# Rotary attention scores on one core: loads that wait for the transposes, a rotation ahead of a copy, an earlier GpSimd drain and fewer semaphores

## The chip, the cores and the metric

One core of one Trainium2 chip runs the kernel. The metric is the device time of one execution in microseconds. Three timed runs of the kernel before gave 801.99, 803.25 and 803.15 us; the median is 803.15.

## The reference

q and k are [16 batches, 512 positions, 16 heads, 64] in float32. Both are rotated by position (rotary embedding), and then the scores of each batch and head are formed between all pairs of positions. The output is [16, 512, 16, 512] float32, which is 268 MB; q and k together are 67 MB.

```python
q_rot = np.concatenate([q1 * cos - q2 * sin, q1 * sin + q2 * cos], axis=-1)   # q1, q2: halves of the last axis
k_rot = np.concatenate([k1 * cos - k2 * sin, k1 * sin + k2 * cos], axis=-1)
scores = np.einsum('bshd,bthd->bsht', q_rot, k_rot)
```

## The kernel before

**Tiles.** A batch of q or of k is one tile of 128 partitions x 4 slots x 1024 numbers (2048 KB); partition p holds positions 4p to 4p+3, and slot c is position 4p+c of all partitions. Two buffers for q and two for k stand in SBUF (`in_t`, L134). The unit of the main loop is one slot of q, numbered i = 4 x batch + slot, 64 in all. For each i the kernel forms all 16 heads' scores in eight head pairs p = 0 to 7 and writes 4096 KB to the output.

**One pass of the main loop (L461 to L485).** TensorE (PE) multiplies a pair's transposed q by the batch's transposed k (`scores`, L343, matmuls on L358). ScalarE (ACT) copies the result out of PSUM into one of three staging buffers (L370), and after the eighth pair SyncE (SP) issues the store of the staging buffer (L382). Between the pairs PE transposes later slots: q's slot i+1 after pairs 1 and 3, k's slot i+4 after pairs 5 and 6 (`transposed`, L287, on L299). VectorE (DVE) copies q's transposes out of PSUM and ACT those of k (L317). DVE rotates q's slot i+2 after pair 3 and k's slot i+5 at the end of the pass (`rope`, L237: three instructions, a product with cos on L275, one with sin in place on L276, their sum on L277). Once a batch DVE copies three of four transposed slots of the next k (kN) into the working k (kT) in two halves: `renew(0)` after pair 3 and `renew(1)` at the end (L325 to L336).

**The first batch (L423 to L458)** is done in another order: its inputs come early in small pieces, its stores are 16 of 1024 KB, and at the end of its last pass (i = 3, L452 to L457) DVE has three things in a row: `renew(1)`, which must wait until PE has made the last pairs of batch 0 since it overwrites their k; the rotation of q's slot 5; and the rotation of k's slot 8.

**Loads.** After pass i with i % 4 = 2 the load of q's batch i/4 + 2 is issued, after i % 4 = 3 that of k's batch i/4 + 3 (L482 to L485). Most go to SP's queue, right behind the store of the same pass, and SP is the only engine that issues stores. Five loads are RELIEVED (L188): q's batches 6, 11 and 15 and k's batches 7 and 12. These are issued by GpSimd (POOL), 120 partitions in 8 KB pieces, with tiny transfers (`move_cursor`) in front that shift which DMA engine takes what; the other 8 partitions go in 2 KB pieces through ACT's queue (q) or POOL's (k) (`load_around`, L199). In the profile SP's queue is q1, POOL's q0, ACT's q10.

**Waits.** `Plan.add` (L30) records which operation reads and writes which key and gives each operation the waits that are not implied by earlier ones; an engine's operations stay in the order in which they are added. A load writes the keys of its tile, so it waits for the tile's readers. The readers on record are the DVE rotations alone: the last is the sum (L277) of the tile's slot 3. Loads on SP's queue stand behind a store which waits for ACT, which is later than all of that; for the five loads on POOL this wait is the one that counts. `place` (L153) gives each operation's semaphore site, one for each engine, parity of i, kind and pair; the PE loop of the main passes counts them up by one a turn.

**The end (L507 to L509).** SP waits for the last stores; POOL waits for the tiny transfers. Then the frame of the program makes each engine drain and meet the others twice, with a clearing of the semaphores by POOL in between (shown at L550).

Of the kernel before, what the change touches and what calls it, by code (L numbers as in the profile page):

```python
# [94 lines left out]
def kernel(  # L95
# [57 lines left out]
    def place(engine, *where):  # L153

        i = now[0]
        return (engine,) + ((i % 2,) + where if i >= C else ("first",))

    def turn():
        i = now[0]
        return (i - FIRST) // 2 if FIRST <= i < FIRST + 2 * TURNS else None  # L160

    def work(engine, fns, reads, writes, *where, aside=False):
        t = turn() if engine == "PE" else None
        plan.add(engine, fns, reads, writes, site=place(engine, *where), turn=t, aside=aside)

# [33 lines left out]
    def load_around(which, b, t, keys, site):  # L199
        n, SMALL = 120, E // 8  # L200
        x = RELIEVED[which, b]
        d = dram[which][b]

        def pieces(queue, lo, hi, F, key, sem):
            m = E // F
            src = bass.AP(d.tensor, d.offset + lo * E + E - F, [(E, hi - lo), (-F, m), (1, F)])
            v = t[lo:hi].rearrange("p c e -> p (c e)")
            dst = bass.AP(v.tensor, v.offset + E - F, [v.ap[0], (-F, m), (1, F)])
            transfer(queue, dst, src, [], [key], sem)

        if x == 0:
            plan.add("POOL", [lambda: nc.gpsimd.inc_swdge_sem([], [], mode="reset_dge_cursor")])
        else:
            move_cursor(16 - SLOW)
        if x % 2:
            move_cursor(8)
            pieces("POOL", n, P, SMALL, keys[1], site + ("rest",))
        move_cursor(SLOW + 1)
        pieces("POOL", 0, n, E // 2, keys[0], site)
        if not x % 2:  # L220
            pieces("ACT", n, P, SMALL, keys[1], site + ("rest",))
# [4 lines left out]
    def load(which, b):  # L226
        if b >= B:
            return
        t, keys = in_t[which, b % 2], in_keys(which, b)
        site = ("in", which, b % 2)  # L230
        if (which, b) in RELIEVED:
            load_around(which, b, t, keys, ("around", which, b))
        else:
            transfer("SP", t.rearrange("p c (h d) -> p c h d", h=H), dram[which][b], [], keys, site)

# [51 lines left out]
    def transposed(which, n, g, engine):  # L287
        j = banks[0] % 2
        banks[0] += 1
        bank = ps_t[j]  # L290
        fns = []
        for x in range(4):
            if n < C:
                src = units[which, n][0][:, x, P * g : P * (g + 1)]
                key = ("unit", which, n)
            else:
                src = rot[which][:, P * (4 * g + x) : P * (4 * g + x + 1)]
                key = ("rot", which)
            fns.append(lambda x=x, src=src: nc.tensor.transpose(bank[:, x, :], src, ident))  # L299
        work("PE", fns, [key, "ident"], [("bank", j)], which, g)  # L300
        src = bank
        if which == "q":
            dst, keys = qT[n % 2][:, 4 * g : 4 * g + 4, :], [("qT", n % 2, g)]
        elif n < C:
            dst = kT[:, 2 * n + g].rearrange("p (t c) -> p t c", c=C)
            src = bank.rearrange("p c t -> p t c")
            keys = [("kT", 2 * n + g, x) for x in range(2)]
        elif n % C < C - 1:
            dst = kN[:, 4 * g : 4 * g + 4, P * (n % C) : P * (n % C + 1)]
            keys = [("kN", n % C, g)]  # L310
        else:
            dst = kT[:, 4 * g : 4 * g + 4, S - P : S]
            keys = [("kT", 4 * g + x, 1) for x in range(4)]

        def copy():
            f = nc.scalar.copy if engine == "ACT" else nc.vector.tensor_copy
            work(engine, [lambda: f(out=dst, in_=src)], [("bank", j)], keys, "out", which, g)  # L317

        return copy
# [23 lines left out]
    def scores(i, p):  # L343
        j = RING[HP * (i % 2) + p]
        s = stage_of(i)
        ps, st = ps_s[j], stage[s]
        b = i // C
        if b == 0:
            c, hp = divmod(p, 2)
            lhs, chunk, g = qT[i % 2][:, C * hp + c], 2 * i + hp, hp  # L350
        else:
            lhs, chunk, g = qT[i % 2][:, p], p, p // 4
        rhs = kT[:, chunk]
        fns = []
        for r in range(2):
            a = slice(64 * r, 64 * r + 64)
            fns.append(
                lambda r=r, a=a: nc.tensor.matmul(  # L358
                    out=ps[:, r, :], lhsT=lhs[a, :], rhs=rhs[a, :], start=True, stop=True
                )  # L360
            )
        work("PE", fns, [("qT", i % 2, g), ("kT", chunk, 0), ("kT", chunk, 1)], [("ps", j)], "pair", p)
        so, si = st[:, 2 * p : 2 * p + 2, :], ps
        if b > 0:
            so = so.rearrange("s r (t c) -> s r t c", c=C)
            si = si.rearrange("s r (c t) -> s r t c", c=C)
        writes = [("st", s, p)]
        if i == 3:
            writes += [("unit", w, n) for w in ("k", "q") for n in range(C)]
        work("ACT", [lambda: nc.scalar.copy(out=so, in_=si)], [("ps", j)], writes, "pair", p)  # L370
        if b == 0 and p % 2 == 1:
            c = p // 2
            transfer(
                "SP",
                o_v[0, c, :, G * i : G * (i + 1)],
                st[:, G * c : G * (c + 1)],
                [("st", s, p - 1), ("st", s, p)],
                [],
                ("store", i, c),
            )  # L380
        elif b > 0 and p == HP - 1:
            transfer("SP", o_v[b, i % C], st, [("st", s, x) for x in range(HP)], [], ("store", s))  # L382

    transfer("ACT", sin_t, sin.rearrange("(p c) j -> p c j", c=C), [], ["sin"], ("sin",))
# [37 lines left out]
    for i in range(C):  # L423
        now[0] = i
        late = []
        for p in range(HP):
            scores(i, p)
            if p in (0, 1) and i > 0:
                if i < C - 1:
                    run(rope("k", i + 1)[2 * p : 2 * p + 2])  # L430
                elif p == 0:
                    run(rope("q", C))
                transposed("k", C + i - 1, p, "DVE")()
            if p == 3 and i < 2:
                load("kq"[i], 2)
            if p == 3 and i == C - 1:
                renew(0)
            if p == 2:
                if i == 0:
                    run(rope("k", 1))  # L440
                tr_act(*(("k", i + 1) if i < C - 1 else ("q", C)))
            if p == 6:
                if i < C - 1:
                    run(rope("q", i + 1))
                    tr_act("q", i + 1)
                else:
                    run(rope("k", C + i))
                    transposed("k", C + i, 0, "ACT")()
                    late.append(transposed("k", C + i, 1, "ACT"))
        for copy in late:  # L450
            copy()
        if i < C - 1:  # L452
            run(rope("k", C + i))
        else:
            renew(1)
            run(rope("q", C + 1))
            run(rope("k", 2 * C))  # L457
    load("k", 3)  # L458

# [42 lines left out]
    with tc.tile_critical(no_gpsimd_drain=True):  # L502
        plan.finish()
        for e in ("SP", "ACT", "POOL", "DVE"):
            for o in plan.ops[e]:
                plan.emit(name[e], o, o.waits.items())
        for s in range(3):  # L507
            nc.sync.wait_ge(plan.sems["store", s], plan.counts["store", s])
        nc.gpsimd.wait_ge(plan.sems[("cursor",)], plan.counts[("cursor",)])  # L509
        for o in ahead_of:  # L510
            plan.emit(nc.tensor, o, o.waits.items())
        levels = sorted({v for _, w in loop for v in w.values()})
        level = {v: nc.tensor.alloc_register(f"level{v}") for v in levels}
        for v in levels:
            nc.tensor.reg_mov(level[v], v)
        with nc.Fori(
            0, TURNS, engines=OrderedEngineSet([mybir.EngineType.PE]), head_slot={mybir.EngineType.PE: 0}
        ):
            for o, w in loop:
                plan.emit(nc.tensor, o, [(site, level[v]) for site, v in w.items()])  # L520
            for v in levels:
                nc.tensor.reg_add(level[v], level[v], 1)
        for o in behind:
            plan.emit(nc.tensor, o, o.waits.items())
# [30 lines left out]
```

## Time and profile before

| | before |
|---|---|
| median of three runs | 803.15 us |
| the profiled execution: its own time, and the span of its trace | 803.83 us, 802.0 us |
| busy PE, DVE, ACT | 681.8, 568.0, 561.9 us |
| moved by DMA, mean rate over the span | 335.84 MB, 419 GB/s |
| ACT's waits for a store to leave its staging buffer | 94.6 us in 24 waits |
| stores: 60 of 4096 KB, median from issue to landing | 23.2 us |
| relieved loads on POOL: q and k, 1920 KB, median from issue to landing | 28.1 us, 43.3 us |

Engines run ahead of one another, so busy time alone says little. The rate of the DMA in a stretch, and who waits for whom at its end, tell what limits it. "Landing" is the time from issue until the completion of a transfer is seen.

### The profile page before, as it was taken

To read this page: it belongs to the slowest core of one execution; us is meant where nothing else is said; L and a number is where in the kernel's file an instruction comes from. 1 tells how busy PE (TensorE), PEld (TensorE's weight loads), DVE (VectorE), ACT (ScalarE), POOL (GpSimd) and SP (SyncE) were. 2 spreads that over 40 slices of the span, in tenths; PEclk is the share of its full clock that TensorE was granted. 3 is DMA by queue.
4 is the path that set the end of the run, shared out by engine and by line. 5 is a ranking of instruction groups with operands and counts; after the bars stand their busy time and mean duration, and the time that the engine had idled before them with its cause. 6 is when DMAs were issued, how large, how long until landed. Compare 5 with 4: busy or idle time off the path is not lost.

```text
span 802.0 us, 7725 instructions
## 1 busy us (share of the span) xinstructions
PE 681.8 (85%) x3072; PEld 296.5 (37%) x3072; DVE 568.0 (71%) x547; ACT 561.9 (70%) x647; POOL 11.8 (1%) x23
## 2 busy tenths in 40 slices
PE   4998999988965999898997984999889898599970
PEld 2444444433422444343343431434334343244420
DVE  7998898857943879685785963879678586488500
ACT  3976887867844888586685862878667686488870
POOL 0000000000000000000000001000000000000000
PEclk9999999999986999898998996999999898799995
DMA  8999999999999999999999999999999999999996
GB/s 340 425 427 413 418 400 430 427 437 425 442 337 433 427 431 432 431 428 438 433 427 438 430 365 434 421 432 428 435 432 424 442 433 387 429 430 433 431 433 293
DMA packets 19079, 335.84 MB, mean 419 GB/s; under 512 B 2376, under 2 KB 3656, under 8 KB 4936
## 3 DMA queue, kind: packets, MB, share of 16 engines
q1 hardware_dynamic: 16288, 324.61, 95.4%
q0 software_dynamic: 1872, 10.10, 3.4%
q10 hardware_dynamic: 904, 0.98, 0.4%
q8 instruction: 4, 0.07, 0.0%
q14 instruction: 11, 0.09, 0.0%
HBM read 67.24 MB, written 268.44 MB: 419 GB/s over the span
## 4 chain that ended last, share of the span: by engine, by line
DMA 44%; PE 42%; ACT 5%; DVE 5%; issue 1%; ACTq 0%; DVEq 0%; SPq 0%
DMA out_dram<-st 44%; PE ps L358 32%; PE bank L299 10%; ACT st L370 5%; DVE st L254 1%; DVE st L251 1%; DVE q_rot L250 1%; DMA st<-in_k_dram 0%; DVE kN_t L317 0%; DVE k_sb L276 0%; DVE q_sb L276 0%; DVE q_rot L277 0%; DVE k_rot L277 0%; DVE q_rot L275 0%; DVE k_rot L275 0%
## 5 line engine op out<-in xcount | busy, mean ns | idle before, releaser
L370 ACT COPY st<-ps 128x1024 f32<-128x1024 f32 x512 | 498.5, 1020 | 204.2 <-PE ps L358 101.7
L358 PE MATMUL ps<-kT_t,qT_t 64*128 64x512 f32 x2048 | 540.1, 645 | 80.0 <-ACT st L370 80.0
L358 PEld LDWEIGHTS ps<-kT_t,qT_t 64*128 64x128 f32 x2048 | 183.0, 195 | 267.7 <-issue 141.3
L317 DVE COPY qT_t<-bank 128x512 f32<-128x512 f32 x118 | 81.1, 687 | 101.6 <-PE bank L299 101.1
L299 PEld LDWEIGHTS bank<-ident,q_rot 128*128 128x128 f32 x480 | 55.0, 150 | 103.7 <-issue 98.0
L299 PE MATMUL bank<-ident,q_rot 128*128 128x128 f32 x480 | 86.2, 307 | 3.9 <-DVE q_rot L277 3.0
L299 PEld LDWEIGHTS bank<-ident,k_rot 128*128 128x128 f32 x480 | 50.3, 140 | 91.7 <-issue 89.2
L275 DVE TENSOR_TENSOR k_rot<-k_sb,cos_t 128x1024 f32<-128x1024 f32 x60 | 73.2, 1220 | 9.9 <-PE bank L299 9.8
L330 DVE COPY kT_t<-kN_t 128x1536 f32<-128x1536 f32 x30 | 28.7, 956 | 71.3 <-PE ps L358 71.3
L299 PE MATMUL bank<-ident,k_rot 128*128 128x128 f32 x480 | 78.5, 286 | 0.1
L276 DVE TENSOR_TENSOR q_sb<-q_sb,ss_t 128x1024 f32<-128x1024 f32 x60 | 73.5, 1226 | 2.0
L277 DVE TENSOR_TENSOR q_rot<-q_rot,q_sb 128x1024 f32<-128x1024 f32 x60 | 73.5, 1225 | 2.1
L277 DVE TENSOR_TENSOR k_rot<-k_rot,k_sb 128x1024 f32<-128x1024 f32 x60 | 73.5, 1225 | 2.1
L276 DVE TENSOR_TENSOR k_sb<-k_sb,ss_t 128x1024 f32<-128x1024 f32 x60 | 73.5, 1225 | 2.0
L275 DVE TENSOR_TENSOR q_rot<-q_sb,cos_t 128x1024 f32<-128x1024 f32 x60 | 72.9, 1215 | 0.0
L317 ACT COPY kN_t<-bank 128x512 f32<-128x512 f32 x84 | 50.1, 597 | 0.0
L317 ACT COPY kT_t<-bank 128x512 f32<-128x512 f32 x38 | 22.3, 596 | 6.4 <-PE bank L299 6.4
L299 PE MATMUL bank<-ident,st 128*128 128x128 f32 x64 | 10.6, 317 | 11.2 <-DVE st L254 11.2
L299 PEld LDWEIGHTS bank<-ident,st 128*128 128x128 f32 x64 | 8.3, 161 | 16.5 <-DVE st L254 10.8
L250 DVE TENSOR_TENSOR q_rot<-st,ss_t 128x1024 f32<-128x1024 f32 x8 | 9.8, 1221 | 4.2 <-DMA st<-in_k_dram 4.1
L167 POOL DMA_DIRECT2D q_sb<-in_q_dram x3 | 2.3, 754 | 618.2 <-DVE q_rot L277 618.2
L254 DVE TENSOR_TENSOR st<-st,q_rot 128x512 f32<-128x512 f32 x16 | 10.3, 687 | 0.2
(14 smaller groups left out, 31.3 us busy)
## 6 DMA issues: line engine op xcount, KB each, us to landing
out_dram<-st SPq DMA_DIRECT2D x60, 4096.0 KB, 23.2
k_sb<-in_k_dram SPq DMA_DIRECT2D x13, 2048.0 KB, 28.6
q_sb<-in_q_dram SPq DMA_DIRECT2D x12, 2048.0 KB, 26.7
out_dram<-st SPq DMA_DIRECT2D x16, 1024.0 KB, 13.7
q_sb<-in_q_dram POOLq DMA_DIRECT2D x3, 1920.0 KB, 28.1
k_sb<-in_k_dram POOLq DMA_DIRECT2D x2, 1920.0 KB, 43.3
st<-in_k_dram SPq DMA_DIRECT2D x1, 1536.0 KB, 9.1
st<-in_q_dram SPq DMA_DIRECT2D x1, 1536.0 KB, 12.1
```

The lines of the kernel that those rows point to most:

```text
L167: plan.add(engine, [lambda: name[engine].dma_start(dst, src)], reads, writes, site=site, transfer=True)
L250: ([lambda: nc.vector.tensor_tensor(pv, xs, ss, op=mult)], keys + ["ss"], [("rot", "q")], unit),
L251: ([lambda: nc.vector.tensor_tensor(xc, xc, cs, op=mult)], keys + ["cos"], [unit] + keys, unit),
L254: lambda y=y: nc.vector.tensor_tensor(x5[:, :, :, y], x5[:, :, :, y], p5[:, :, :, 1 - y], op=add)
L275: ([lambda: nc.vector.tensor_tensor(yc, xc, cs, op=mult)], ["cos"] + keys, [("rot", which)], which + "_cos"),
L276: ([lambda: nc.vector.tensor_tensor(xs, xs, ss, op=mult)], ["ss"], keys, which + "_sin"),
L277: ([lambda: nc.vector.tensor_tensor(y4, y4, swapped, op=add)], keys, [("rot", which)], which + "_sum"),
L299: fns.append(lambda x=x, src=src: nc.tensor.transpose(bank[:, x, :], src, ident))
L317: work(engine, [lambda: f(out=dst, in_=src)], [("bank", j)], keys, "out", which, g)
L330: [lambda: nc.vector.tensor_copy(out=dst, in_=src)],
L358: lambda r=r, a=a: nc.tensor.matmul(out=ps[:, r, :], lhsT=lhs[a, :], rhs=rhs[a, :], start=True, stop=True)
L370: work("ACT", [lambda: nc.scalar.copy(out=so, in_=si)], [("ps", j)], writes, "pair", p)
```

## The change

Four edits. (1) The transposes of a tile's last slot (slot 3) count as readers of the tile, so that its reload waits for PE's second group of those transposes and no longer for DVE's sum. For the loads on SP's queue nothing new results. POOL's loads wait: q's batch 6 for the second group of transposes of q's slot 19, which PE makes after pair 3 of pass 18 (before: the sum of slot 19, on DVE in pass 17); q's 11 and 15 likewise in passes 38 and 54; k's 7 and 12 for the second group of k's slots 23 and 43, after pair 6 of passes 19 and 39 (before: the sums at the ends of passes 18 and 38). (2) At the end of pass 3, q's slot 5 is rotated ahead of `renew(1)`. (3) POOL waits for its tiny transfers and drains in its own stream, ahead of the frame's drains. (4) Only ACT's score copies and DVE's q copies and q sums keep semaphores by parity and pair; all else of an engine shares one, stores of a staging buffer share theirs, and so do all relieved loads of q, or of k. The plan's sites fall from 100 to 53 by their names in the programs (the change's note counts 58). The order of the other instructions stays; PE has one more wait, for `renew(1)` ahead of pair 4 of pass 4.

```diff
     def place(engine, *where):
 
         i = now[0]
-        return (engine,) + ((i % 2,) + where if i >= C else ("first",))
+        own = engine == "ACT" and where[0] == "pair" or engine == "DVE" and where[0] in ("out", "q_sum")
+        return (engine, i % 2) + where if own and i >= C else (engine,)
...
         if (which, b) in RELIEVED:
-            load_around(which, b, t, keys, ("around", which, b))
+            load_around(which, b, t, keys, ("around", which))
...
-        work("PE", fns, [key, "ident"], [("bank", j)], which, g)
+        held = in_keys(which, n // C) if n >= C and n % C == C - 1 else []
+        work("PE", fns, [key, "ident"] + held, [("bank", j)], which, g)
...
-                ("store", i, c),
+                ("store", s, c),
...
-            transfer("SP", o_v[b, i % C], st, [("st", s, x) for x in range(HP)], [], ("store", s))
+            transfer("SP", o_v[b, i % C], st, [("st", s, x) for x in range(HP)], [], ("store", s, 0))
...
         else:
+            run(rope("q", C + 1))
             renew(1)
-            run(rope("q", C + 1))
             run(rope("k", 2 * C))
...
+        nc.gpsimd.wait_ge(plan.sems[("cursor",)], plan.counts[("cursor",)])
+        nc.gpsimd.drain()
         for s in range(3):
-            nc.sync.wait_ge(plan.sems["store", s], plan.counts["store", s])
-        nc.gpsimd.wait_ge(plan.sems[("cursor",)], plan.counts[("cursor",)])
+            nc.sync.wait_ge(plan.sems["store", s, 0], plan.counts["store", s, 0])
```

More of the change, by code (lines that the diff above doesn't have):

```diff
@@ L162, in work @@
     def work(engine, fns, reads, writes, *where, aside=False):
+        where = where or ("",)
         t = turn() if engine == "PE" else None
```

## The prediction

> **What bounds the kernel now.** I read the page first: its span, the DMA's line in 40 slices, and the chain that ended last; then who waited for whom.
>
> ```profile
> span 802.0 us, 7725 instructions
> DMA  8999999999999999999999999999999999999996
> DMA 44%; PE 42%; ACT 5%; DVE 5%; issue 1%; ACTq 0%; DVEq 0%; SPq 0%
> ACT st L370 <- DMA out_dram<-st: 94.6, 24, 12.3
> ```
>
> The DMA engines are busy from the second slice to the last but one, and ACT stands still for 94.6 us in 24 waits for stores to leave a staging buffer. So compute has time to spare and DMA bounds the kernel. The chain's 42% on PE is no contradiction: between two such waits the chain runs through PE at its own pace. Time is therefore won only where the DMA moves fewer bytes per second than it can. The windows show where (their last two columns are DMA share and GB/s).
>
> ```profile
> 78.00:139.00 61.00, 61.00 (x293) 26.69 (x292) 53.36 (x52) 52.81 (x62) 0.00 (x0) 1.00 0.99 411
> 139.00:222.00 83.00, 73.96 (x344) 31.83 (x344) 64.35 (x62) 60.95 (x70) 1.89 (x3) 0.98 1.00 432
> 222.00:237.00 15.00, 10.22 (x40) 4.38 (x40) 6.61 (x6) 8.59 (x10) 0.00 (x0) 0.77 1.00 309
> 256.00:281.00 25.00, 25.00 (x120) 10.79 (x119) 21.64 (x21) 21.39 (x26) 0.00 (x0) 1.00 1.02 435
> 281.00:470.00 189.00, 172.91 (x776) 74.77 (x776) 143.77 (x138) 139.57 (x161) 1.88 (x3) 0.94 1.00 431
> 470.00:483.00 13.00, 10.91 (x44) 4.25 (x44) 7.72 (x8) 8.67 (x10) 0.00 (x0) 0.87 1.03 338
> 530.00:669.00 139.00, 127.79 (x576) 55.12 (x576) 107.03 (x102) 103.83 (x120) 0.75 (x1) 0.95 1.00 432
> 669.00:680.00 11.00, 8.36 (x27) 3.14 (x25) 4.44 (x5) 6.37 (x7) 0.00 (x0) 0.69 1.02 360
> ```
>
> Long stretches run at 431 or 432 GB/s, loads and stores mixed. Three short ones fall to 309, 338 and 360 while the DMA share stays at 1: the engines are occupied, but their packets take longer. A fourth, 78 to 139 us, is a little low at 411, with PE busy all the time.
>
> **Edit 1, the later relieved loads.** What happens in the three dips? Each begins a few us after a relieved load of q is issued (the POOL rows), and each time a load of k on SP's queue is on the way. Around the first (the issues in order of time, and between them, from the DMA view of 199.6 to 200.4 us, size and us from issue to landing of the two on SP's queue):
>
> ```profile
> 199.49 0.33 SPq L167 DMA_DIRECT2D out_dram<-st  x1
> 199.86 0.85 SPq L167 DMA_DIRECT2D k_sb<-in_k_dram  x1
> out_dram<-st SPq DMA_DIRECT2D x1, 4096.0 KB, 26.1
> k_sb<-in_k_dram SPq DMA_DIRECT2D x1, 2048.0 KB, 37.3
> 217.92 0.76 POOL L167 DMA_DIRECT2D q_sb<-in_q_dram  x1 [215.25 <-DVE q_rot L277]
> 239.81 0.76 POOL L167 DMA_DIRECT2D k_sb<-in_k_dram  x1
> 467.08 0.75 POOL L167 DMA_DIRECT2D q_sb<-in_q_dram  x1 [225.38 <-DVE q_rot L277]
> 665.21 0.75 POOL L167 DMA_DIRECT2D q_sb<-in_q_dram  x1 [177.59 <-DVE q_rot L277]
> ```
>
> The store of pass 15 lands at 199.5 + 26.1 = 225.6, the load of k right behind it at 199.9 + 37.3 = 237.2. Its 2.1 MB had the queue for 11.6 us; at 432 GB/s they need 4.9. The two queues, inside the dip (225 to 235) and beside a relieved load of k, with no load on SP's queue (265 to 275):
>
> ```profile
> q1 hardware_dynamic: 119, 1.93, 67.7%
> q0 software_dynamic: 122, 0.93, 31.5%
> q1 hardware_dynamic: 120, 3.41, 79.6%
> q0 software_dynamic: 107, 0.88, 20.7%
> ```
>
> In the dip 1.93 MB took 67.7% of 16 engines for 10 us, 17.8 GB/s an engine; in the other window 3.41 MB took 79.6%, 26.8 GB/s. The relieved load moves as many bytes beside stores (0.88 MB) as in the dip (0.93), and there costs nothing (the window 256 to 281 has 435). So I read the dips as two loads into SBUF at once, from two queues, which slow each other; one load beside stores doesn't. The dip ends when the load of k does.
>
> Now the edit. q's load 6 will wait for PE's second group of q's slot 19, in pass 18:
>
> ```profile
> 225.71 2.84 ACT L370 COPY st<-ps 128x1024 f32<-128x1024 f32 x3 [5.73 <-DMA out_dram<-st]
> 228.79 1.11 PE L299 MATMUL bank<-ident,q_rot 128*128 128x128 f32 x4
> 257.47 0.66 PE L299 MATMUL bank<-ident,k_rot 128*128 128x128 f32 x4
> 300.59 1.22 DVE L275 TENSOR_TENSOR k_rot<-k_sb,cos_t 128x1024 f32<-128x1024 f32 x1
> ```
>
> That group ends at 228.8 + 1.1 = 229.9, 12 us after the issue before, at 217.9. It cannot come sooner than the staging buffer: pair 3 needs a PSUM bank that ACT empties only after the store of pass 15 has landed (225.7). The load of k stands right behind that store and needs 4.9 us alone; the relieved load is issued 4.3 us after that landing and its first bytes come later still (before, the dip begins some 4 us after the issue). So the two no longer overlap, by the order of the queues and not by luck. Loads 11 and 15 stand in passes 38 and 54, which have the same place in the batch and the same turn of the staging buffers. If the dips go, the gain is what was not moved: (432 - 309) x 15 / 432 = 4.3 us, (432 - 338) x 13 / 432 = 2.8, (432 - 360) x 11 / 432 = 1.8, together **8.9 us**. Bounds: 0, if the slow packets go along with the relieved load wherever it is put, and 10 (an estimate: by the 435 of the row beside stores the sum is 9.1, and the windows may cut off the dips' edges).
>
> What is late next? Behind the waiting load on POOL stand the tiny transfers and k's load 7. That waits for k's slot 23, whose second group ends at 257.5 + 0.7 = 258.1, not for the sum before 239.8: 18 us later, less what has been gained by then (2.5 from edit 2 and 4.3), so at about 251. From the page, issue to landing:
>
> ```profile
> q_sb<-in_q_dram POOLq DMA_DIRECT2D x3, 1920.0 KB, 28.1
> k_sb<-in_k_dram POOLq DMA_DIRECT2D x2, 1920.0 KB, 43.3
> k_sb<-in_k_dram SPq DMA_DIRECT2D x13, 2048.0 KB, 28.6
> ```
>
> q's load lands at 229.9 - 2.5 + 28.1 = 255.5 instead of 246.0. Before, k's lands at 239.8 + 43.3 = 283.1, 37.1 us after q's, since both share queue 0. Kept, that is 292.6. Its reader, the rotation of k's slot 28, stands at 300.6 - 6.8 = 293.8. That just holds, by 1.2 us; and were it some us late, DVE would stand still ahead of `renew(1)` and PE at pair 4 of pass 24, with stores and a load of k (28.6 us to landing) queued: some 17 us of cover (estimated as 28.6 less one pass of 10 us and 2 us of latency). I take the cost as nothing.
>
> **Edit 2, the rotation ahead of the copy.** Timeline at the end of pass 3, and the same groups of PE in a settled pass:
>
> ```profile
> 62.48 0.96 DVE L330 COPY kT_t<-kN_t 128x1536 f32<-128x1536 f32 x1 [2.87 <-PE ps L358]
> 67.14 1.11 PE L299 MATMUL bank<-ident,q_rot 128*128 128x128 f32 x4 [3.00 <-DVE q_rot L277]
> 71.25 0.42 PEld L299 LDWEIGHTS bank<-ident,q_rot 128*128 128x128 f32 x4 [0.85 <-issue]
> 78.77 0.66 PE L299 MATMUL bank<-ident,q_rot 128*128 128x128 f32 x4
> 81.27 0.66 PE L299 MATMUL bank<-ident,q_rot 128*128 128x128 f32 x4
> ```
>
> DVE idles 2.87 us ahead of the copy, then PE idles 3.00 us for the rotation behind it, and its next group follows after 4.1 us and not 2.5, for its clock has dropped. With the rotation first, it starts 2.9 us sooner and skips the copy's 0.96; PE finds it done. The copy, then at about 63.3, is in time for pair 4 of pass 4 (the added wait). PE gains up to 3.0 + 1.6 = 4.6 us, the next stores as much. What does DMA make of it? The stretch 78 to 139 is where compute sets the pace. It lacks (432 - 411) x 61 / 432 = 3.0 us, and stores 4.6 us sooner can fill that at most. I take **2.5**, near the upper end as the shift exceeds the shortfall; bounds 0 and 3.0.
>
> **Edit 3 and the semaphores: the end.**
>
> ```profile
> SPq L508 <- DMA out_dram<-st: 20.3, 1, 20.3
> L550 POOLq DRAIN  x3: 40/223/1529, 799.1 to 801.8; - x3
> L550 SPq DRAIN  x3: 7/7/7, 799.4 to 800.9; - x3
> L550 POOLq EVENT_SEMAPHORE_RANGE_CLEAR  x1: 612/612/612, 801.1 to 801.1; - x1
> ```
>
> At the end POOL drains three times; the first, at 799.1, takes 1529 ns, and the others meet it only then: SP is there at 799.5, POOL at 800.7. If POOL has drained long before, the first should cost like the others, 40 to 223 ns: **1.2 us** gained; 0, if the time is not that of the loads. The clearing (612 ns) covers 59 semaphores, not 106: 0 to 0.27 us, I take 0.1. The rest of edit 4 costs nothing: waits and order stay, and the added increments lie on engines that wait for DMA.
>
> **The sum.** 8.9 + 2.5 + 1.2 + 0.1 = 12.7 us. The profiled execution took 803.8 us (802.0 of span and 1.8 around it), 0.7 above the median; 803.15 - 12.7 = 790.4, and I forecast **790.5 us**.
>
> **The rivals.**
> - *The overlap is free* (12%). If loads from two queues merely interleave, the dips have another cause and stay: 803.15 - 3.8 = 799.3. For it: no stretch shows queue 0 and SP's loads apart from relieved loads of q. Against it: the dip follows the load of k, not that of q. The Trainium skill (DMA: Bandwidth & Descriptors, "Issuing engines are not separate DMA queues") says that transfers issued from several engines interleave on the same 16 DMA engines; by that rule this rival wins, but the trace, with 309 GB/s at a full share, disagrees.
> - *Half of it* (8%): the relieved loads still meet the tail of k's load, or their wait moves the dips; half of 8.9 remains: 795.
> - *Slower* (7%): queue 0 starves beside stores. The later q load now runs beside stores alone. If each relieved load took 16 us longer there, k's load 7 would land 32 us later, at 325, 31 after its reader; beyond the 17 of cover 14 are lost, and again at load 12: 28 - 12.7 = 15 us slower, 818. It decides from about 12 us longer each. Against it: 0.88 MB in 10 us beside stores.
> - *It doesn't do it* (3%): POOL's wait was not what held the load, and the early drain not the long one: within 0.2% of before.
>
> **How the numbers follow.** My forecast has 70%, from 787.5 (3.0 + 10 + 1.5 gained, and 1.2 for the scatter of the runs shown, 801.99 below a median of 803.15) to 794. With the half case and the free overlap 90% lies below 799.5; the range 787.5 to 799.5 leaves out 10% at the slow side and some beyond my bounds. A measurement of this kernel can tell about 0.2% (1.6 us) from no change. Faster: 70 + 12 + 8 = 90%; same 3%; slower 7%.
>
> **What would show it.** Right: no window of 10 us below 400 GB/s at the three places; POOL's q loads issued about 10 us later, each behind the landing that frees ACT; SP's load of k landing some 5 us after its store; PE without a stall of 3 us at 64; POOL's first closing drain under 0.3 us. Wrong: dips that move along with the relieved loads; DVE waiting for k's load at 294 or 537; a stretch 78 to 139 that stays at 411.

## The result, and the profile after

The kernel after takes **793.35 us** (median of 6 runs, 792.72 to 793.68), beside 801.36 us for the kernel before in the same comparison (6 runs, 797.83 to 803.25): a ratio of **0.9902, 95% interval 0.9878 to 0.9926**, by which it is 7.9 us faster (5.9 to 9.8; the two medians differ by 8.0). The profiled execution took 793.32 us (before 803.83), its span went from 802.0 to 791.4. Direction and range of the forecast held (790.5, 787.5 to 799.5); the sum of 12.7 us was too large.

The same rows as before: the span and DMA's line on the page, and from the waits ACT's for the stores.

```profile
span 791.4 us, 7726 instructions
DMA  8999999999999999999999999999999999999996
```

```profile
ACT st L373 <- DMA out_dram<-st: 91.2, 33, 6.7
```

DMA still bounds it: busy in all but the first and the last slice, and ACT waits nearly as long in total (91.2 us, before 94.6), but in shorter pieces (longest 6.7, before 12.3). The windows (last two columns: DMA share, GB/s), with one more, 300 to 310, and the tail:

```profile
78.00:139.00 61.00, 57.77 (x276) 24.97 (x272) 51.38 (x49) 48.34 (x56) 0.00 (x0) 0.99 1.01 433
222.00:237.00 15.00, 11.46 (x54) 4.64 (x52) 9.69 (x10) 8.69 (x10) 1.89 (x3) 1.00 1.02 439
300.00:310.00 10.00, 10.00 (x51) 4.41 (x49) 8.45 (x8) 8.67 (x11) 0.00 (x0) 1.00 0.99 374
470.00:483.00 13.00, 12.97 (x48) 5.00 (x46) 8.55 (x8) 7.48 (x9) 1.88 (x3) 0.77 1.01 434
669.00:680.00 11.00, 6.62 (x32) 2.83 (x32) 6.58 (x6) 4.88 (x7) 0.00 (x0) 1.00 0.97 416
782.00:790.00 8.00, 0.00 (x0) 0.00 (x0) 0.00 (x0) 0.00 (x0) 0.00 (x0) 0.50 0.34 147
```

The three dips are gone (439, 434 and 416 for 309, 338 and 360), and so is the shortfall from 78 to 139 (433 for 411). By the trace's packet records, no packet of a load on SP's queue moves any more while one of the five relieved loads does. New are a dip at 300 to 310 (374), and a thin tail: for the last 8 us the engines are busy for a third. In the kernel before, 300 to 310 was hardly disturbed and the tail was shorter:

```profile
300.00:310.00 10.00, 10.00 (x50) 4.42 (x48) 9.60 (x10) 8.68 (x11) 0.00 (x0) 1.00 0.97 418
784.00:792.00 8.00, 0.00 (x0) 0.00 (x0) 0.00 (x0) 0.00 (x0) 0.00 (x0) 0.50 1.01 434
792.00:799.00 7.00, 0.00 (x0) 0.00 (x0) 0.00 (x0) 0.00 (x0) 0.00 (x0) 0.50 0.52 225
```

Edit 1 at work, around q's batch 6: from the timeline POOL's two issues and the reader of the second load, on DVE,

```profile
226.57 0.76 POOL L169 DMA_DIRECT2D q_sb<-in_q_dram  x1 [223.90 <-PE bank L301]
248.85 0.76 POOL L169 DMA_DIRECT2D k_sb<-in_k_dram  x1
292.26 1.23 DVE L277 TENSOR_TENSOR k_rot<-k_sb,cos_t 128x1024 f32<-128x1024 f32 x1
```

and from the DMA view the us from issue to landing, of the store and the load of k on SP's queue (issued 200.9 and 201.2), then of the two relieved loads.

```profile
out_dram<-st SPq DMA_DIRECT2D x1, 4096.0 KB, 22.5
k_sb<-in_k_dram SPq DMA_DIRECT2D x1, 2048.0 KB, 27.0
q_sb<-in_q_dram POOLq DMA_DIRECT2D x1, 1920.0 KB, 28.6
k_sb<-in_k_dram POOLq DMA_DIRECT2D x1, 1920.0 KB, 41.7
```

POOL now waits for PE. SP's load of k lands at 228.2, 4.8 us after its store (before 11.6), 3 us ahead of the relieved load's first packets (231.2). That one lands at 255.2, k's at 290.6, and k's reader on DVE starts at 292.3 without a wait. Edit 2 at the end of pass 3 (timeline), and the closing (the instructions of one line: shortest, median and longest ns, first and last start):

```profile
61.62 1.22 DVE L279 TENSOR_TENSOR q_rot<-q_rot,q_sb 128x1024 f32<-128x1024 f32 x1
62.77 0.95 DVE L333 COPY kT_t<-kN_t 128x1536 f32<-128x1536 f32 x1
63.66 0.42 PEld L301 LDWEIGHTS bank<-ident,q_rot 128*128 128x128 f32 x4 [0.76 <-DVE q_rot L279]
63.67 0.66 PE L301 MATMUL bank<-ident,q_rot 128*128 128x128 f32 x4
```

```profile
L554 POOLq DRAIN  x3: 34/47/150, 790.0 to 791.1; - x3
L554 POOLq EVENT_SEMAPHORE_RANGE_CLEAR  x1: 355/355/355, 790.7 to 790.7; - x1
```

PE no longer idles for the rotated slot (before 3.00 us): its transposes start at 63.67, as the matmuls ahead of them end. Only the weight load (PEld) idles 0.76 us ahead of them, and that is what it also idles ahead of the next group of transposes, where it waits for nothing. POOL's longest closing drain takes 150 ns, not 1529, the clearing 355 ns, not 612.

**Where the sum fell short in this pair of executions.** The trace has 16 raises of the semaphore for every store, each with a time of its own. I take them for the landings of the 16 DMA engines, one each; the trace doesn't number the engines. Worked out from them, for the last store (us):

```
              first   mean    last    span's end
before        794.3   796.5   798.8   802.0
after         783.1   785.6   789.7   791.4
```

The mean engine gained 10.9 us, close to the 11.4 that the forecast gave edits 1 and 2. The last engine gained 9.1, and the kernel ends with the last: it is 4.1 us behind the mean now, and was 2.3. From there to the end of the span it went from 3.2 to 1.7 us. So 10.9 - 1.8 + 1.5 = 10.6 us, the difference of the spans. The pair gained 10.6 us, the comparison of six runs each 7.9; that remainder is taken up with the experiments. Of the 10.9 us, 3.7 are gained ahead of the first relieved load (mean landing of pass 12's store: 189.2 before, 185.5 after).

### The profile page after: what moved, and what is told of

Same layout as the page of the kernel before. It is cut to its first block, busy times and chain, and to the rows that moved or that the text cites. A ratio compares the mean times of both kernels' runs of the same rounds, so it can differ in the third digit from the quotient of the medians.

```text
span 791.4 us, 7726 instructions
## 1 busy us (share of the span) xinstructions
PE 687.7 (87%) x3072; PEld 296.8 (37%) x3072; DVE 568.2 (72%) x547; ACT 562.1 (71%) x647; POOL 11.7 (1%) x23
## 4 chain that ended last, share of the span: by engine, by line
DMA 46%; PE 42%; ACT 4%; DVE 4%; issue 1%; ACTq 0%; DVEq 0%; SPq 0%
DMA out_dram<-st 46%; PE ps L361 32%; PE bank L301 10%; ACT st L373 4%; DVE st L256 1%; DVE st L253 1%; DVE q_rot L252 1%; DMA st<-in_k_dram 0%; DVE kN_t L320 0%; DVE k_sb L278 0%; DVE k_rot L279 0%; DVE k_rot L277 0%; DVE q_sb L278 0%; DVE q_rot L279 0%; DVE q_rot L277 0%
## 5 line engine op out<-in xcount | busy, mean ns | idle before, releaser
L361 PE MATMUL ps<-kT_t,qT_t 64*128 64x512 f32 x2048 | 546.2, 650 | 68.2 <-ACT st L373 68.2
L301 PE MATMUL bank<-ident,st 128*128 128x128 f32 x64 | 10.6, 317 | 11.0 <-DVE st L256 11.0
L301 PEld LDWEIGHTS bank<-ident,st 128*128 128x128 f32 x64 | 8.3, 161 | 16.2 <-DVE st L256 10.6
```

What stands on the lines that cost most here:

```text
L361: lambda r=r, a=a: nc.tensor.matmul(out=ps[:, r, :], lhsT=lhs[a, :], rhs=rhs[a, :], start=True, stop=True)
```

## The experiments

Theory: two loads into SBUF at once, from two queues, slow each other; edit 1 keeps them apart; the last of the 16 DMA engines sets the end. Rivals: the form of the relieved load, and not that two loads overlap, makes the dips; the gain is that of the other edits; the mean pace counts and not the last engine. A drop below 432 GB/s is turned into time as in the forecast: (432 - rate) x length / 432.

**Each edit by itself** (one chip; before 801.94 us there, 23 runs).

*Edit 1 alone.*

```diff
-        work("PE", fns, [key, "ident"], [("bank", j)], which, g)
+        held = in_keys(which, n // C) if n >= C and n % C == C - 1 else []
+        work("PE", fns, [key, "ident"] + held, [("bank", j)], which, g)
```

> The kernel before with edit 1 alone: loads also wait for the transposes of slot 3. Theory (two loads on two queues slow each other): no dip in the three places, where before the DMA fell to 309, 338 and 360 GB/s; 6 to 9 us faster than before, with POOL's first closing drain still near 1.5 us. Rival (the slow packets belong to the relieved load wherever it stands): dips of the same size some 10 us later, and no gain. Rival (half): dips of half the size, 4 us.

Measured: 798.43 us, ratio 0.996 (0.9944 to 0.9976). Its three stretches, 300 to 310, and 78 to 139:

```profile
222.00:237.00 15.00, 12.25 (x52) 4.85 (x49) 9.02 (x10) 8.79 (x10) 1.89 (x3) 0.89 1.00 429
470.00:483.00 13.00, 11.11 (x40) 4.62 (x40) 6.59 (x6) 8.67 (x10) 1.88 (x3) 0.74 0.99 429
669.00:680.00 11.00, 8.35 (x40) 3.33 (x38) 8.28 (x8) 5.70 (x7) 0.75 (x1) 0.97 0.98 419
300.00:310.00 10.00, 10.00 (x51) 4.41 (x50) 8.46 (x8) 8.73 (x11) 0.00 (x0) 1.00 1.00 395
78.00:139.00 61.00, 59.91 (x288) 26.16 (x284) 53.29 (x52) 50.23 (x58) 0.00 (x0) 1.00 1.00 428
```

Moving the loads is enough to remove the dips, and it brings the new one at 300 to 310. The gain is 3.5 us by the medians (3.2 by the ratio, 1.9 to 4.5), and not the 8.9 of the forecast or the 6 to 9 expected. The execution shown took 795.45 us, 3 less than the median, and that is in part not edit 1's doing: without edit 2 it runs from 78 to 139 at 428 GB/s, where the profiled execution of before had 411, and (428 - 411) x 61 / 432 = 2.4 us.

*All but edit 1* (the kernel after with the line of `work("PE", ...)` as before).

> The changed kernel without edit 1: the rotation, the drain and the fewer semaphores stay. Theory: the three dips are back, and 2.5 to 4 us remain of the gain. Rival (the dips went for another reason, such as the shift of the first passes or the shared semaphores): no dips, and the whole gain of 8 to 10 us.

Measured: 796.92 us, ratio 0.9948 (0.993 to 0.9966), so edit 1 on top of the rest is worth 0.9902 / 0.9948, 0.5% or 3.7 us (by the two intervals, give or take 2.4). The rest is worth 4.2 us by the ratio, just above the 2.5 to 4 expected. The dips come earlier as everything does; each window is moved with its dip:

```profile
218.00:233.00 15.00, 12.70 (x54) 5.37 (x52) 9.47 (x9) 8.88 (x12) 1.89 (x3) 0.89 1.00 379
464.00:477.00 13.00, 11.50 (x56) 4.72 (x52) 9.64 (x10) 9.91 (x12) 1.08 (x2) 1.00 1.04 384
661.00:672.00 11.00, 7.87 (x24) 2.92 (x23) 4.70 (x6) 4.87 (x5) 0.00 (x0) 0.69 1.03 353
```

They cost 1.8 + 1.4 + 2.0 = 5.3 us here.

*Edit 2 alone.*

```diff
         else:
+            run(rope("q", C + 1))
             renew(1)
-            run(rope("q", C + 1))
```

> The kernel before with edit 2 alone: q's slot 5 rotated ahead of the second copy. Theory: PE's stall of 3.0 us at 64 us goes, the stretch 78 to 139 us rises from 411 towards 430 GB/s, 1.5 to 2.5 us faster. Rival (one slow DMA engine sets the end, and idled less than the others in that stretch): the stretch rises, but the landing of the last engine comes less than 1 us sooner, and so does the end.

Measured: 798.87 us, ratio 0.9959 (0.9941 to 0.9977), a gain of 3.1 us by the medians (1.8 to 4.7 by the interval); the stretch 78 to 139 runs at 433 GB/s. What there is to gain differs from one execution to the next: in the eight profiled executions of this document without edit 2 that stretch runs at 411 to 428 GB/s (0.6 to 3.0 us lost), in the six with it at 431 to 435. The forecast read it from the lowest of the eight. The three dips, in windows moved as above, run at 391, 375 and 329 GB/s and cost 5.8 us.

*Edit 3 alone.*

```diff
+        nc.gpsimd.wait_ge(plan.sems[("cursor",)], plan.counts[("cursor",)])
+        nc.gpsimd.drain()
         for s in range(3):
             nc.sync.wait_ge(plan.sems["store", s], plan.counts["store", s])
-        nc.gpsimd.wait_ge(plan.sems[("cursor",)], plan.counts[("cursor",)])
```

> The kernel before with edit 3 alone: GpSimd waits for its tiny transfers and drains in its own stream. Theory: the first closing drain of GpSimd falls from 1529 ns to under 300 ns, and the time by 1.2 us. Rival (the drain is long because GpSimd has long been idle, not because of its loads): 1.5 us as before, no gain.

Measured: 801.48 us, ratio 0.9982 (0.9961 to 1.0002): the times alone leave it open, but the trace shows it. First its own drain and the frame's, then the dips:

```profile
L508 POOLq DRAIN  x1: 29880/29880/29880, 664.6 to 664.6; - x1
L551 POOLq DRAIN  x3: 34/47/223, 798.4 to 799.8; - x3
```

```profile
222.00:237.00 15.00, 11.86 (x50) 4.98 (x48) 8.63 (x9) 8.81 (x11) 0.30 (x1) 0.89 1.01 355
470.00:483.00 13.00, 10.38 (x44) 4.18 (x42) 7.18 (x8) 8.39 (x10) 0.00 (x0) 0.87 1.03 367
669.00:680.00 11.00, 8.92 (x36) 4.06 (x38) 5.67 (x6) 7.65 (x9) 0.00 (x0) 0.84 1.01 401
```

The drain now waits for the last relieved load at 664.6, where nobody waits for POOL. From the last landing to the span's end: 800.1 - 798.0 = 2.1 us, 1.1 less than before. Nothing in this kernel touches the dips, and they cost 2.7 + 2.0 + 0.8 = 5.4 us in it. So three executions lose 5.3 to 5.8 us to the dips; the 8.9 of the profiled execution of before was large.

**Does the last engine set the time?** The kernel after without relieved loads: `RELIEVED = {}`, and no wait for tiny transfers at the end.

> The kernel after, with no relieved load: all loads are plain ones of 128 partitions on SP's queue, none on GpSimd's, and GpSimd's closing wait for them is gone. Theory 1 (the time is set by the DMA engine that finishes last, and one engine is slower): in the traces so far one of the 16 landings of each store falls behind the median of its store by about 1 us per batch; without relief it keeps falling, to some 14 us behind the mean of the 16 at the last store. The mean itself has no overlapping loads any more and can gain the 3.1 us that the kernel after still has above a pace of 48.5 us per batch: the mean of the last store's landings 782.5, the last 797, the time 799 to 801. Theory 2 (the mean pace of the 16 engines sets the time, one engine's lag is made up by the others): time 788 to 791, the last landing at most 5 us behind the mean.

Measured: 801.43 us, ratio 1.0 to before (0.9984 to 1.0015). All that the change gained is lost again, though none of the windows read from 222 to 310 is below 422 GB/s. The two last windows:

```profile
780.00:790.00 10.00, 0.00 (x0) 0.00 (x0) 0.00 (x0) 0.00 (x0) 0.00 (x0) 0.58 1.05 455
790.00:800.00 10.00, 0.00 (x0) 0.00 (x0) 0.00 (x0) 0.00 (x0) 0.00 (x0) 0.50 0.08 36
```

For the last 10 us 8% of the engines' time is busy: about one of 16. By the landings the last engine is 3.9 us behind the mean at the store of pass 16 and 11.5 at that of pass 52, nine batches later: 0.84 us a batch. The last but one is 1.8 behind there, so it is one engine. Then ACT waits 3.6 us for that engine (at 719.8), the DMA share falls to 0.66 and 0.82 in the two windows from 720 to 740, and the lag is 6.5 at the end. So the theory holds in its order of events: the slowest engine sets the time, and the five relieved loads are worth 8 us to the kernel after. Its details were off: the lag was to grow to 14 and the mean landing of the last store to come at 782.5; it came at 792.1, since the others had stood waiting, and the time is just above the 799 to 801 expected.

**What makes the dips?** *The five loads plain* (128 partitions, no tiny transfers and no closing wait for them) on GpSimd's queue, at the places of before:

```diff
-            load_around(which, b, t, keys, ("around", which, b))
+            transfer("POOL", t.rearrange("p c (h d) -> p c h d", h=H), dram[which][b], [], keys, ("around", which, b))
```

> The kernel before, with its five relieved loads issued at the same places on GpSimd's queue, but as plain loads of all 128 partitions, without the tiny transfers that shift partitions to other DMA engines. Theory 1 (two loads into SBUF at once, from two queues, slow each other, whatever their form): the stretch 222 to 237 stays below 400 GB/s, likewise those near 470 and 669. Theory 2 (the shifted partitions are what collides: one engine then serves other partitions than with SP's loads): no stretch there below 425. Total time is not the measure: without relief one DMA engine falls behind, so 800 to 815 by either.

Measured: 805.34 us, ratio 1.0045 (1.0026 to 1.0064). One window, and both queues in the middle of the overlap, 223 to 229 (packets, MB, share):

```profile
222.00:237.00 15.00, 12.26 (x46) 4.92 (x44) 7.70 (x8) 8.37 (x10) 0.00 (x0) 0.77 1.01 435
```

```profile
q1 hardware_dynamic: 101, 1.57, 61.2%
q0 software_dynamic: 63, 1.03, 40.1%
```

*The same with q's loads on ACT's hardware queue*, issued behind pair 6 of passes 17, 37 and 53 (`transfer("ACT" if which == "q" else "POOL", ...)`).

> The kernel before with its five relieved loads as plain loads of 128 partitions, those of q issued on ACT's hardware queue at the place in time where GpSimd issued them (behind pair 6 of passes 17, 37 and 53), those of k on GpSimd's. Theory 1 (any two loads from two queues at once slow each other): 222 to 237 below 400 GB/s as with GpSimd's queue. Theory 2 (it is GpSimd's software queue that makes a load slow beside another): no stretch below 425 at the three places although q's and k's loads overlap. Total time is not the measure (no relief: 800 to 815).

Measured: 804.59 us, ratio 1.0051 (1.0025 to 1.0077); ACT's queue is q10.

```profile
q10 hardware_dynamic: 81, 1.33, 51.6%
q1 hardware_dynamic: 81, 1.29, 50.3%
```

In both, two loads run at once and nothing slows: 2.60 and 2.62 MB in 6 us, 434 and 437 GB/s. By the packet records nearly every 16 KB packet of both takes 611 ns while the two overlap; in the first dip of before, half of those on SP's queue take 997 or more. **My mechanism falls**: two loads at once from two queues do share the engines without loss. It must be the form of the relieved load. Its parts: the tiny transfers, which are to shift it to other engines, the small pieces, the 120 partitions.

*The relieved form unshifted* (before, `SLOW = 15` for `SLOW = 4`: other sizes of the tiny transfers, and with the same 120 partitions, 8 KB pieces and places), and *plain loads shifted* (the plain loads on GpSimd's queue, ahead of the first a tiny transfer of 5 partitions).

> [...] Theory 1 (the dips come from the shift: two engines at the same group of partitions, one for each load): no dip, 222 to 237, 470 to 483 and 669 to 680 above 420 GB/s, though both loads are on the way as in the kernel before. Theory 2 (they come from the form of the relieved load, its small pieces or their order): dips of 309 to 370 GB/s as before. By theory 1 the median engine gains some 9 us, but the slow engine isn't relieved, falls some 10 us behind and takes it away: time 797 to 804.

> [...] Theory 1 (the shift is the cause): the dips come back, 222 to 237, 470 to 483 and 669 to 680 below 400 GB/s, packets of the two loads 1.3 to 1.7 times as long. Theory 2 (the form of the relieved load): no stretch below 420, as without the tiny transfer. Time 803 to 815 by theory 1 (no relief and the dips), 803 to 807 by theory 2.

Measured: 814.2 us (ratio 1.0162, 1.0123 to 1.0202) and 804.01 us (1.0028, 1.0001 to 1.0056). Queues from 223 to 229, unshifted first:

```profile
q1 hardware_dynamic: 83, 1.54, 71.9%
q0 software_dynamic: 79, 0.59, 31.2%
```

```profile
q1 hardware_dynamic: 80, 1.41, 54.7%
q0 software_dynamic: 77, 1.26, 49.0%
```

The unshifted relieved load still slows SP's (2.13 MB, 355 GB/s; at the two later places only 6 and 8 of the 128 packets of SP's load were left when the relieved load began), the shifted plain ones don't (2.67 MB, 445). That either run moves the loads to the engines it was meant to is assumed: the trace doesn't number the engines. If it does, the shift is not needed for the loss, and it alone does not make one. The unshifted kernel is 11 us slower (797 to 804 us expected). That fits a relief that misses the slow engine: the last landing is 14.7 us behind the mean at the store of pass 36, where it is 8.7 in the kernel without relief.

*Whole pieces*: before, and the kernel after without edit 1, with relieved loads in pieces of 16 KB.

```diff
-        pieces("POOL", 0, n, E // 2, keys[0], site)
+        pieces("POOL", 0, n, E, keys[0], site)
```

> The kernel before with one constant changed: the relieved loads move each partition in one piece of 16 KB, as plain loads do, and not in two of 8 KB from the back; 120 partitions, the shift to DMA engine 5, places and waits stay. Theory 1 (a load slows another only if its pieces are small: plain loads of 16 KB pieces did not, shifted or not, and the unshifted one of 8 KB pieces did): no dips, the three stretches above 420 GB/s while both loads are on the way, packets of 16 KB at their usual 611 ns, and the gain of edit 1 alone without edit 1: 797.5 to 799. Theory 2 (the 120 partitions on 15 engines collide): dips of 309 to 400 GB/s as before, 801 to 803.

> The kernel after without edit 1 (loads don't wait for the transposes), with relieved loads in pieces of 16 KB instead of 8 KB. If all that edit 1 does is to keep the small pieces of a relieved load away from SP's load (theory 1), whole pieces do the same without it: no dips, and the time of the kernel after, 792.5 to 794. If edit 1 gained by something else as well, or whole pieces relieve the slow engine less: 795 to 798, as without edit 1 (796.92). A faster version than both kernels only if the stretch near 300 to 310 us, 374 GB/s in the kernel after and undisturbed without edit 1, also stays clean: then 791 to 792.5.

Measured: 819.28 us (ratio 1.0231, 1.0195 to 1.0267) and 817.63 us (1.0193, 1.0155 to 1.023). Of the first, the window and the queues from 223 to 229:

```profile
222.00:237.00 15.00, 12.81 (x62) 5.11 (x58) 11.01 (x11) 9.39 (x12) 1.29 (x3) 1.00 1.03 319
```

```profile
q1 hardware_dynamic: 74, 1.20, 64.7%
q0 software_dynamic: 43, 0.62, 40.8%
```

The dip is there with whole pieces, so small pieces are not needed either. By the trace's packet records a packet of 16 KB takes 611 ns undisturbed; from 222 to 232 here half of those on GpSimd's queue take 1101 or more. The second kernel, which also has edit 2, runs at 261 GB/s in the same window. So of what sets the relieved load apart, the 120 partitions are in every run with a dip; no run has 120 partitions with neither the shift nor the small pieces, so it may be that one of these two must come with them. Such a load leaves one engine out: in before, one of the 16 landings of pass 20's store comes at 283.9, the other 15 from 290.4 to 292.6.

The Trainium skill (DMA: Bandwidth & Descriptors, "The descriptor swizzle") states that in a transfer of 128 partitions each engine writes the eight partitions of one SBUF port, two groups of four that lie 32 apart. By that rule two plain loads never meet at a port, since the engine that owns it takes their packets in turn. If 120 partitions were dealt out in 15 runs of eight neighbours, each engine would write to two ports and each port would have two engines. That would give what these runs show: no loss for plain beside plain (434 to 445 GB/s), a loss for 120 beside 128 (261 to 355). But it would also let the engines of one relieved load meet each other, and they don't slow down: beside stores, in before from 256.5 to 281, an 8 KB packet of it runs together with 6.8 others on average, and all 240 take 309 to 313 ns. So ports in that form don't explain the dips, and how the 120 are dealt out isn't in the trace. The mechanism stays open.

That both kernels are over 15 us slower I had not foreseen. In the first, one landing of pass 18's store is 14 us ahead of the median, and the last one still fell behind the median (2.3 us at pass 14, 5.4 at 18, 15.5 at 52). With one piece for each partition, it follows, another engine was left out than the slow one. The Trainium skill (DMA: Bandwidth & Descriptors, "Why a DMA increments its semaphore by 16 and not by 1") has an exception that would do this: some direct copies on GpSimd's queue are split as for all 16 engines, a sixteenth of the partitions rounded up for each. Worked out from it, 120 partitions would go, eight each, to the engines 0 to 14, whatever tiny transfers went ahead; no run here shows engine numbers. The whole pieces also change more than the size: of the 120 packets of k's relieved load from 253 to 269, beside stores alone, 31 take over 5% longer than 611 ns. Whether whole pieces could stand in for edit 1 is thus not answered.

**Which loads have to wait?** The kernel after, with only q's three relieved loads held:

```diff
-        held = in_keys(which, n // C) if n >= C and n % C == C - 1 else []
+        held = in_keys(which, n // C) if which == "q" and ("q", n // C + 2) in RELIEVED and n % C == C - 1 else []
```

> The kernel after, in which only the three relieved loads of q wait for the transposes of their slot; the relieved loads of k and all plain loads go out as in the kernel before. Theory 1 (the whole of edit 1's gain comes from q's three loads): the three stretches stay above 425 GB/s and the time is that of the kernel after, 792 to 794. Theory 1b: the dip of the kernel after at 300 to 310 us (374 GB/s, behind k's relieved load, which lands at 293 there and at 284 where it isn't held) goes away with the earlier load of k, and its counterpart near 545: up to 1.9 us less, 791 to 792.5. Rival (k's loads and the plain ones also had to be held): dips of under 400 GB/s come back somewhere between 220 and 300, and the time is 795 to 797.

Measured: 793.3 us, ratio 0.9901 (0.9879 to 0.9922): that of the kernel after.

```profile
300.00:310.00 10.00, 10.00 (x50) 4.41 (x50) 8.46 (x8) 8.68 (x11) 0.00 (x0) 1.00 0.98 372
```

Edit 1's whole gain comes from three loads, and k's later load 7 costs nothing and isn't what makes the dip at 300: that stays (372). It comes with the held load of q: 374, 395 and 372 in the three kernels that hold it, 418 to 428 in before and in those with edit 2 or 3 or all but edit 1. No load on GpSimd's queue is on the way then. What slows down are packets of one plain load of q on SP's queue: from 300 to 312, 37 of its 128 in the kernel after take over 700 ns instead of 611 (35 here), in the kernels without the hold one or two. So packets of a load can also stretch without a second load, and why is open.

## Why the forecast was right, and where its size was not

*What bounds the kernel, and the direction*: right. DMA bounds it, and time came from stretches in which it moved less.

*Edit 1, the order of events*: right nearly to the microsecond. q's load issued at 226.6 (forecast 229.9 - 2.5 = 227.4), landed at 255.2 (255.5), k's at 290.6 (292.6), its reader at 292.3 (293.8), 1.7 us of room (1.2). The slower rival, with queue 0 starving, did not come. In part the half rival did: less than half of edit 1's term was left, and a dip came up elsewhere, though not beside a relieved load.

*Edit 1, the reason*: right that the three dips need both loads at once, since either apart from the other runs clean there. Wrong as "two loads into SBUF at once, from two queues, which slow each other": the runs with plain loads overlap at 434 and 437 GB/s. There the rule of the Trainium skill (DMA: Bandwidth & Descriptors, "Issuing engines are not separate DMA queues"), by which transfers from several issuing engines interleave on the same DMA engines, agrees with the trace; for the load of 120 partitions beside one of 128 it is not the whole story (309).

*Edit 1, the size*: **this is the step that failed**, 8.9 us for 3.5 alone and 3.7 on top of the rest. Three reasons. (a) The dips were sized in one execution, the only one profiled, which took 803.83 us where before has a median of 801.36 beside the kernel after; in three other executions in which the relieved loads weren't held they cost 5.3 to 5.8. I subtracted the dips of a long execution from a median. (b) With the held load of q comes a dip at 300 to 310, (432 - 374) x 10 / 432 = 1.3 us. (c) The terms went by the rate of all 16 engines, while the last one ends the kernel. In before the dips hold up 15 engines and spare the one left out (at the store of pass 20 it is 7 us ahead of the median); without them the mean gains more than the last engine does, in the profiled pair by 1.8 us, which belong to all the edits together. (a) and (b) alone leave 5.5 - 1.3 = 4.2 us. That (c) takes the rest, down to the 3.5 to 3.7 measured, is not shown, and the intervals are wider than that rest.

*Edit 2*: 2.5 forecast, 3.1 measured alone (0.23% to 0.59%, 1.8 to 4.7 us); the stall and the shortfall went as told. But the shortfall, too, was read from an execution in which it was large: 3.0 us, of 0.6 to 3.0 in eight.

*Edit 3 and the semaphores*: 1.2 and 0.1 forecast; 1.1 and 0.26 by the traces. The upper bound of the second was the right value: the clearing took 612 ns, and 355 with 47 semaphores fewer. That the first closing drain is long because of GpSimd's loads was right, but it is so long after they have landed, too, and goes by their number (last section).

*The sum*, by what was measured: 3.7 + 3.1 + 1.1 + 0.3 = 8.2 us, beside 7.9. The first two are each uncertain by 1.5 to 2.4 us, and the close agreement says little. And that the time came within 3 us of the forecast, with a gain that was forecast 4.8 too large, is in part luck: the sum was taken off the median of three runs, 803.15, which lies 1.8 above that of six.

## What to carry to other kernels

Before a dip in one profile is priced, look at the scatter of the runs: in an execution 0.3% above the median just this dip can be larger, as it was here, and a sum made from it shouldn't be subtracted from the median. Where 16 DMA engines work side by side, the mean rate says what was gained and the last landing when the kernel ends; look at the tail window and the 16 landings of the last store. And a cause read from one coincidence (two loads at once) wants one run that keeps the coincidence and changes the form.

## What the runs showed of the hardware

One DMA engine of the 16 is slower than the rest: without relief it falls 0.84 us behind a batch of 48.5 us, 1.7% (a batch is four stores and two loads; in that run the mean landings of the stores of passes 24 and 28 lie 48.5 us apart). A load of 120 partitions beside one of 128 makes both slow (303 and 355 GB/s over 223 to 229 us, 309 over 222 to 237 in before), two of 128 do not (434 to 445), whether from GpSimd's queue and SP's or from ACT's and SP's; beside stores the load of 120 costs nothing (435). Which engine such a load leaves out seems to hang on its pieces: with 16 KB for 8 KB the slow one wasn't relieved, and 17.5 us were lost.

GpSimd's first closing drain goes by the number of transfers that GpSimd issued. Two rows of the closing lines, the first with five plain loads on GpSimd's queue, the second with those five and one tiny transfer:

```profile
L549 POOLq DRAIN  x3: 34/204/464, 800.0 to 801.6; - x3
L553 POOLq DRAIN  x3: 40/211/545, 798.8 to 800.4; - x3
```

The longest is the first in time: 464 ns with 5 transfers and 545 with 6, 217 with the 2 of the run with q's loads on ACT's queue, and 1529 with the 18 of before. That is 82 ns for each more (545 - 464 = 81, (1529 - 545) / 12 = 82), over 100 us after the last of them has landed. The drain of edit 3, alone, stands right behind the issue of the last load (664.6) and takes 29.9 us: it ends 0.8 us after that load has landed (693.7). The closing drains behind it take 0.03 to 0.22 us.
